# Queueing the small TensorE products of a hybrid decoder kernel and issuing them singly

## The chip, the cores and the metric

The kernel runs on one core of one Trainium2 chip. The metric is the device time of one execution in microseconds, of the slowest core (there is one). Three runs of the kernel before took 1936.96, 1938.45 and 1943.08 us; their median is 1938.45 us.

## The reference, cut to what matters

A trunk of two decoder layers over 1024 tokens of width 1024, in float32. Cut to its frame:

```python
for l in range(DEPTH):                       # DEPTH = 2
    h = x * (1 + scale1) + shift1            # scale, shift, gate: c_act @ ada_w[l]
    if l % 2 == 0:
        y = _even_mixer(h, ...)              # 4 gated-recurrence heads + windowed attention, 8 query heads
    else:
        y = _pool_mixer(h, ...)              # trailing means over 2, 4, 8, 16 tokens
    x = _layer_norm(ALPHA * x + g1 * y, ...)
    h = x * (1 + scale2) + shift2
    y = _conv_ffn(h, ...)                    # (silu(conv3(u)) * v) @ w_down, width 2816
    x = _layer_norm(ALPHA * x + g2 * y, ...)
```

The even mixer multiplies h by one input matrix, runs a chunkwise gated linear recurrence (128 keys by 128 values a head) and an attention over a window of 128 tokens beside each other, and maps both results by an output matrix.

## The kernel before, in words

The tokens are split in two halves of 512 (`NH = 2`, index `hf`), and each half in four tiles of 128 (`NT`). **Large products** are those with weights from memory. Each float32 operand is split into a high and a low part (`split`, L296 to L297: ACT casts the high part, DVE subtracts the low one), and three passes (`PASSES`) are summed in PSUM. They stand in `gemm` (L306, 128x512 each), `tok_products` (L430, 128x256), the value and gate part of `head_in` (L532, 128x256), `product` (L999, up-projection in a form with fewer products) and `down` (L1145).

**Small products** are those of 128x128 or less, in plain float32: in `mixer_head` the scores of a chunk at eight levels (`att`, L775, by `level`), transposes of the keys (`ktp`, L808), state updates (`up`, L817) and outputs (`ho`, L833 and L835); `join_head` transposes a head's output (`ogT`, L862); in `mixer_swa` transposes of keys, queries and probabilities (`kp` L636, `qp` L648, `tpz` L716); in `layer_norm` the variance (`varp`, L357, one column) and the transpose that spreads the reciprocal root (`rstd`, L365). Each comes in a group of four, one for each tile of 128 tokens or each head of a pair; `up` is three or four, `ho` four and then three or four. In the trace a small product of two operands is two MATMUL records and a transpose is one. The attention's scores (`sc`, L673) and values (`op`, L733) are small too, and the change leaves them as they are.

**The order of the work** is written out by hand with Python generators. A chain (`swa_chain`, one `head_chain` for each head and half, `norm_prep`, `between`, `last`) yields after each step; `start` puts it on the list `active` with a rate. The large products call `tick` at fixed places: in `gemm` after 9, 18 and (by `outproj` or `head_in`) 24 of 24 products, in the value part of `head_in` after each 24. At a tick every active chain gains its rate and takes one step for each whole unit: rate 1 for attention, 0.9 for a head, 3 for `norm_prep(0)`. A step places its group of four, and right behind it the DVE or ACT instruction that reads the result. The stages are: input projections of half 0, of half 1 (chains of half 0 beside them), `finish` for the chains of half 0, `outproj(0)` (192 large products, 24 ticks, chains of half 1 beside them), `finish` for those, `outproj(1)` with `norm_prep(0)` beside it, and then for each layer `early`, `paired`, `down(0)` and `down(1)`. `finish(gen)` runs what is left of a chain to its end, with nothing between.

The framework below the code places instructions on each engine by the code's order and by when it expects their operands, so an engine's order can differ from the code's. It sets all semaphores. PSUM is two pools of four banks: `mm` for large products, `ax` for small ones. Temporary tiles come from pools of 512 columns: `t2` (19 buffers) and `e2` (6).

Of the kernel before, what the change touches and what calls it, by code (L numbers as in the profile page):

```python
# [1 line left out]

# [1 line left out]

# [47 lines left out]
AHEAD = 2  # L52
KEEP = 5
PIN = 1
EARLY = (16, 22)
EARLY_CONV = (0, 12)
FILL = 0.65
# [4 lines left out]
def trunk(ctx: ExitStack, tc: tile.TileContext, a: dict, out: bass.AP):  # L62
# [34 lines left out]
    active = []  # L97

    def start(gen, rate):
        active.append([gen, rate, 0])  # L100
        return gen

    def tick():
        for item in list(active):
            item[2] += item[1]
            while item[2] >= 1:
                item[2] -= 1
                with ExitStack() as order:
                    for i in behind:
                        order.enter_context(tc.issue_after(i.ins))  # L110
                    over = next(item[0], active) is active
                if over:
                    active.remove(item)
                    break

    def finish(gen=None, keep=0):
        if gen is not None:
            for _ in gen:
                pass
            active[:] = [x for x in active if x[0] is not gen]  # L120
        else:
            while len(active) > keep:
                for _ in active.pop(0)[0]:
                    pass


    def load(name, shape, dt=F32, src=None):
# [197 lines left out]
    def layer_norm(r, w=HT, s=None):  # L325
        if s is None:
            s = t2("lns")[:, :w]
            V.tensor_tensor(s, r[0], r[1], ALU.add)
            for j in range(2, KT):
                yield  # L330
                V.tensor_tensor(s, s, r[j], ALU.add)
            yield
        mu = ax("mu")[:, :w]
        if w < HT:
            PE.matmul(mu, mean_w.bitcast(F32), s, start=True, stop=True)
        else:
# [19 lines left out]
        for tt in range(nt):  # L356
            PE.matmul(vp[:, tt : tt + 1], ss[:, tt * P : (tt + 1) * P], mean_c, start=True, stop=True)  # L357
# [6 lines left out]
        for tt in range(nt):  # L364
            PE.transpose(bp[:, tt * P : (tt + 1) * P], y[:, tt : tt + 1].broadcast_to([P, P]), ident)  # L365
        yield
        for j in range(KT):
            V.tensor_tensor(r[j], r[j], bp, ALU.mult)
            yield
# [58 lines left out]
    def tok_products(ps, w, h, k, t, first, last):  # L428
        for pi, (wi, hi) in enumerate(PASSES):
            PE.matmul(  # L430
                ps[t // 2][:, (t % 2) * 256 : (t % 2 + 1) * 256],
                h[k][:, hi, t * P : (t + 1) * P],
                w[wi][:, (k % 4) * 256 : (k % 4 + 1) * 256],
                start=first and pi == 0 and t % 2 == 0,
                stop=last and pi == 2 and t % 2 == 1,
            )

    def swa_tiles(hf):
        z = [b4(f"z{g}_{hf}").rearrange("p (t c) -> p t c", t=NT) for g in range(3)]
# [61 lines left out]
    def head_in(hd, hf, pf=None):  # L501
# [24 lines left out]
        for t in range(0, NT, 2):  # L526
            ps = mm("zt")
            for u in range(2):
                i = 0
                for k_ in range(KT):  # L530
                    for wi, hi in PASSES:
                        PE.matmul(  # L532
                            ps[:, u * 256 : (u + 1) * 256],
                            h[k_][:, hi, (t + u) * P : (t + u + 1) * P],
                            w[k_ // 4][wi][:, (k_ % 4) * 256 : (k_ % 4 + 1) * 256],
                            start=i == 0,
                            stop=i == 23,
                        )
                        i += 1
                if u == 0:  # L540
# [86 lines left out]
    def mixer_swa(z, hf):  # L627
# [4 lines left out]
        rope(z[1], 4, hf)  # L632
        yield
        kp = ax("kp")
        for t in range(NT):
            PE.transpose(kp[:, t * P : (t + 1) * P], z[2][:, t, 0:P], ident)  # L636
        kT = t2("kT")
        S.copy(kT, kp)
        kTs[hf], vv_ = kT, t2("vv").rearrange("p (t c) -> p t c", t=NT)
# [4 lines left out]
        yield  # L644
        def queries(t):
            qp = ax("qp")
            for j in range(4):
                PE.transpose(qp[:, j * P : (j + 1) * P], z[j // 2][:, t, (j % 2) * P : (j % 2 + 1) * P], ident)  # L648
            qT = t2("qT")
            S.copy(qT, qp)  # L650
            return qT
# [59 lines left out]
        def turn(t, kv, p):  # L711
            r = []
            for kb in (1,) if hf * NT + t == 0 else (0, 1):
                tpz = ax("tpz")
                for j in range(4):
                    PE.transpose(tpz[:, j * P : (j + 1) * P], p[:, j, kb * P : (kb + 1) * P], ident)  # L716
                pT = t2("pT")
                if kb:
                    V.tensor_copy(pT, tpz)
# [21 lines left out]
        qT = queries(0)  # L741
        yield
        for t in range(NT):
            cur = yield from scores(t, qT)
            yield
            if prev is not None:
                parts = turn(t - 1, 0, prev[0])
                yield
                parts += turn(t - 1, 1, prev[1])
                yield  # L750
            if t < NT - 1:
                qT = queries(t + 1)
# [5 lines left out]
        parts = turn(NT - 1, 0, prev[0])  # L758
        yield
        parts += turn(NT - 1, 1, prev[1])  # L760
        yield
        yield
        values(NT - 1, parts)
# [1 line left out]

    def mixer_head(st, hd, hf):
        f, K, q, Q, z = st
        tot = t2("tot")
        att = t2("att")

        def level(lhs, rhs):
            ps = ax("att")
            for c in range(NT):
                s = slice(c * P, (c + 1) * P)
                PE.matmul(ps[:, s], lhs[:, s], rhs[:, s], start=True, stop=True)  # L775
            return ps

        ps = level(K, q)
# [7 lines left out]
        cur, off = f, 0  # L786
        for li, m in enumerate(LEVELS):
            nb = HT // (2 * m)
            ps = level(K, Q)
# [14 lines left out]
            yield  # L804

        kp = ax("ktp")
        for c in range(NT):
            PE.transpose(kp[:, c * P : (c + 1) * P], K[:, c * P : (c + 1) * P], ident)  # L808
        kt = q
        S.copy(kt, kp)  # L810
        yield
        yield
        up = ax("up")
        for c in range(NT):
            if hf == NH - 1 and c == NT - 1:
                continue
            PE.matmul(up[:, c * P : (c + 1) * P], kt[:, c * P : (c + 1) * P], z[:, c, 0:P], start=True, stop=True)  # L817
        st_in = [states.get(hd)]
        for c in range(NT):
            if hf == NH - 1 and c == NT - 1:  # L820
# [7 lines left out]
        states[hd] = st_in[-1]  # L828
        yield
        op = ax("ho")  # L830
        for c in range(NT):
            s = slice(c * P, (c + 1) * P)
            PE.matmul(op[:, s], att[:, s], z[:, c, 0:P], start=True, stop=st_in[c] is None)  # L833
            if st_in[c] is not None:
                PE.matmul(op[:, s], Q[:, s], st_in[c], start=False, stop=True)  # L835
            if c == 1:
                yield
        ssq = sm([P, NT], "ssq", 2)
        junk = sm([P, P], "junk", 1)
        for c in range(NT):  # L840
# [16 lines left out]
    def join_head(hf, hd):  # L857
        o = o_hl[hf]
        ps = ax("ogT")
        for c in range(NT):  # L860
            s = slice(c * P, (c + 1) * P)
            PE.transpose(ps[:, s], og[hf, hd][:, s], ident)  # L862
        split(o[hd][:, 0, :], o[hd][:, 1, :], ps)

    def join_swa(hf):
# [13 lines left out]
    def head_chain(st, hd, hf):  # L879
        yield from mixer_head(st, hd, hf)  # L880
        yield
        while o_hl[hf] is None:
            yield
        join_head(hf, hd)
        yield

    rs_ = [None, None]
# [108 lines left out]
    def product(ps, w, blk, start, stop):  # L996
        for k in range(HK):
            for pi, (wi, hi) in enumerate(PASSES):
# [2 lines left out]
                    start=start and k == pi == 0, stop=stop and k == HK - 1 and pi == 2,  # L1001
                    skip_group_check=True,
                )
            if k == 1:
                tick()
        fill()
# [110 lines left out]
    def down(l, hf):  # L1117
# [15 lines left out]
        for j0 in range(0, KT, 2):  # L1133
# [4 lines left out]
            for c0, nk in CHUNKS[:2] if final else CHUNKS:  # L1138
                w = [weight("w_dn", l, hf, j, c0, nk) for j in (j0, j0 + 1)]
                for k in range(c0, c0 + nk):  # L1140
                    while len(g) < min(FP, k // 2 + 3):
                        load_hidden()
                    for jj in range(2):
                        for pi, (wi, hi) in enumerate(PASSES):
                            PE.matmul(  # L1145
                                ps[jj], w[jj][wi][:, (k - c0) * P : (k - c0 + 1) * P], act(k, hi),
                                start=k == pi == 0, stop=k == sum(last_k) - 1 and pi == 2,
                            )
                    tick()
                    if k % 4 == 3:  # L1150
                        fill()
# [220 lines left out]
```

## Time and profile before

| | |
|---|---|
| median of three runs | 1938.45 us |
| profiled execution | 1934.68 us |
| its span, first to last instruction | 1932.9 us |
| mean granted TensorE clock | 0.991 of full |
| PE busy | 1866.4 us (97%) |
| DVE busy | 1389.3 us (72%) |
| ACT busy | 897.4 us (46%) |

PE is TensorE's matmuls, PEld its weight loads, DVE is VectorE, ACT ScalarE. All durations below come from this one profiled execution, whose span is 1.8 us shorter than its own time. A matmul's recorded duration is modelled and overlaps that of the next one; the chain of waits gives each piece the time up to the next piece, and so shows what a group really takes on the engine.

### The profile page before, as it was taken

What the parts mean: (1) busy time and instruction counts of PE and PEld (TensorE: products, weight loads), DVE (VectorE), ACT (ScalarE), POOL (GpSimd) and SP (SyncE); (2) the same over time, 40 slices, a digit from 0 to 9 for tenths busy, and PEclk for the clock granted to TensorE, in tenths of its full rate; (3) what the DMA queues carried; (4) which work ended last, traced back from release to release, by engine and by line L of the source; (5) the groups of instructions that cost most, each with busy time, mean ns of one, the idle gap of its engine ahead of it and who ended that gap; (6) DMA issues with size and microseconds to landing.
All of it is one profiled execution on the core that took longest, in us unless ns stands there. A gap on an engine that the chain in (4) does not pass through costs nothing.

```text
span 1932.9 us, 25673 instructions
## 1 busy us (share of the span) xinstructions
PE 1866.4 (97%) x9390; PEld 1553.2 (80%) x9390; DVE 1389.3 (72%) x2651; ACT 897.4 (46%) x1408; POOL 0.2 (0%) x4
## 2 busy tenths in 40 slices
PE   6999999999998999999999999997999999999996
PEld 5988988898776888888888888885888888888886
DVE  6897677787789888887634784898887776634506
ACT  4764245433676444444522644656645443423522
POOL 0000000000000000000000000000000000000000
PEclk9999999999999999999999999998999999999998
DMA  8722332224777666554676757457644444867861
GB/s 312 243 96 87 110 110 94 92 100 143 248 264 281 236 222 236 205 180 153 234 271 231 279 176 275 145 186 272 231 151 152 147 155 154 286 232 255 321 213 44
DMA packets 139087, 377.98 MB, mean 196 GB/s; under 512 B 17104, under 2 KB 19536, under 8 KB 138960
## 3 DMA queue, kind: packets, MB, share of 16 engines
q1 hardware_dynamic: 126288, 353.78, 52.3%
q10 hardware_dynamic: 12672, 22.55, 3.1%
q8 instruction: 74, 1.21, 0.3%
q14 instruction: 53, 0.43, 0.1%
HBM read 289.24 MB, written 87.03 MB: 195 GB/s over the span
## 4 chain that ended last, share of the span: by engine, by line
PE 83%; DVE 8%; DMA 4%; ACT 2%; issue 2%; SPq 0%; DVEq 0%; ACTq 0%
PE pd L1145 23%; PE py L999 18%; PE pz L999 12%; PE px L999 9%; PE zt L532 4%; PE op L306 3%; PE att L775 3%; DMA adast<-in_ada_wT 2%; PE zt L430 2%; PE pd L306 2%; DVE whl L297 1%; PE aq L306 1%; PE pp L1231 1%; DVE adast L152 1%; PE af L306 1%
## 5 line engine op out<-in xcount | busy, mean ns | idle before, releaser
L999 PE MATMUL py<-t,whl 128*128 128x512 f32 x1584 | 374.5, 392 | 5.6 <-ACT whl L297 1.9
L999 PEld LDWEIGHTS py<-t,whl 128*128 128x128 f32 x1584 | 296.4, 188 | 75.6 <-DVE v L1109 3.3
L297 ACT CAST whl<-wst 128x1024 fp32r<-128x1024 f32 (+1 forms) x196 | 200.3, 1033 | 283.8 <-PE pd L1145 114.2
L1145 PE MATMUL pd<-gh,whl 128*128 128x512 f32 x1024 | 319.7, 390 | 0.0
L297 DVE TENSOR_TENSOR whl<-wst,whl 128x1024 fp32r<-128x1024 f32 (+1 forms) x196 | 233.1, 1199 | 104.8 <-ACT whl L297 104.1
L999 PE MATMUL px<-hf,whl 128*128 128x512 f32 x1056 | 254.0, 397 | 20.1 <-ACT uh L952 14.0
L999 PEld LDWEIGHTS px<-hf,whl 128*128 128x128 f32 x1056 | 201.0, 191 | 65.4 <-ACT uh L952 15.7
L1145 PEld LDWEIGHTS pd<-gh,whl 128*128 128x128 f32 x1024 | 192.0, 188 | 40.1
L1145 PE MATMUL pd<-gl,whl 128*128 128x512 f32 x512 | 199.4, 389 | 0.0
L152 DVE CUSTOM_DVE_ANT_0 adast<-adast,c 128x1024 f32<-128x1024 f32 x96 | 117.2, 1221 | 41.8 <-DMA adast<-in_ada_wT 41.5
L999 PE MATMUL pz<-t,whl 128*128 128x512 f32 x528 | 130.3, 395 | 0.0
L999 PE MATMUL pz<-hf,gs 128*128 128x512 f32 x528 | 129.1, 393 | 0.0
L999 PEld LDWEIGHTS pz<-t,whl 128*128 128x128 f32 x528 | 99.2, 188 | 23.6
L999 PEld LDWEIGHTS pz<-hf,gs 128*128 128x128 f32 x528 | 99.1, 188 | 22.7
L1145 PEld LDWEIGHTS pd<-gl,whl 128*128 128x128 f32 x512 | 96.1, 188 | 20.2
L1145 PE MATMUL pd<-gt,whl 128*128 128x512 f32 x432 | 103.3, 395 | 0.0
L532 PE MATMUL zt<-whl,h 128*128 128x256 f32 x768 | 100.6, 286 | 0.0
L953 ACT ACTIVATE uc<-uc 128x512 f32<-128x512 f32 x88 | 55.8, 634 | 91.9 <-DVE uc L948 76.1
L1155 DVE SCALAR_TENSOR_TENSOR r<-pd,mod,r 128x512 f32<-128x512 f32 x32 | 23.1, 750 | 104.6 <-PE pd L1145 104.6
L1145 PEld LDWEIGHTS pd<-gt,whl 128*128 128x128 f32 x432 | 80.7, 187 | 20.3 <-DVE gt L297 0.5
L946 DVE SCALAR_TENSOR_TENSOR uc<-u,cw,uc 128x511 f32<-128x511 f32 x124 | 92.4, 745 | 5.4 <-ACT uc L943 5.2
L532 PEld LDWEIGHTS zt<-whl,h 128*128 128x128 f32 x768 | 94.4, 191 | 0.7 <-issue 0.3
(244 smaller groups left out, 2694.9 us busy)
## 6 DMA issues: line engine op xcount, KB each, us to landing
wst<-in_w_up SPq DMA_DIRECT2D x126, 512.0 KB, 4.3
adast<-in_ada_wT SPq DMA_DIRECT2D x96, 512.0 KB, 3.9
wst<-in_w_dn SPq DMA_DIRECT2D x64, 512.0 KB, 5.6
wst<-g SPq DMA_DIRECT2D x44, 512.0 KB, 5.2
r<-r SPq DMA_DIRECT2D x64, 256.0 KB, 3.9
wl<-whl SPq DMA_DIRECT2D x32, 512.0 KB, 3.1
whl<-wl SPq DMA_DIRECT2D x32, 512.0 KB, 4.6
g<-uc SPq DMA_DIRECT2D x62, 256.0 KB, 2.0
```

The source lines that it names most:

```text
L152: V.tensor_tensor_reduce(out=w, in0=w, in1=cb, scale=1.0, scalar=0.0, op0=ALU.mult, op1=ALU.add, accum_out=col(mods[l, ch], k),)
L297: return S.copy(hi, src), V.tensor_tensor(lo, src, hi.bitcast(F32), ALU.subtract)
L306: PE.matmul(ps, w[wi][:, k * P : (k + 1) * P], act(k, hi), start=i == 0, stop=i == n - 1)
L430: PE.matmul(ps[t // 2][:, (t % 2) * 256 : (t % 2 + 1) * 256], h[k][:, hi, t * P : (t + 1) * P], w[wi][:, (k % 4) * 256 : (k % 4 + 1) * 256 ...
L532: PE.matmul(ps[:, u * 256 : (u + 1) * 256], h[k_][:, hi, (t + u) * P : (t + u + 1) * P], w[k_ // 4][wi][:, (k_ % 4) * 256 : (k_ % 4 + 1) * ...
L775: PE.matmul(ps[:, s], lhs[:, s], rhs[:, s], start=True, stop=True)
L946: V.scalar_tensor_tensor(uc[:, sh:], u[:, : HT - sh], cw, uc[:, sh:], ALU.mult, ALU.add)
L953: S.activation(uc, uc, AF.Silu)
L999: PE.matmul(ps, w[wi][:, k * P : (k + 1) * P], blk[k][hi], start=start and k == pi == 0, stop=stop and k == HK - 1 and pi == 2, skip_group ...
L1145: PE.matmul(ps[jj], w[jj][wi][:, (k - c0) * P : (k - c0 + 1) * P], act(k, hi), start=k == pi == 0, stop=k == sum(last_k) - 1 and pi == 2,)
L1155: V.scalar_tensor_tensor(n[j], ps[jj], col(mods[l, 5], j), n[j], ALU.mult, ALU.add)
L1231: PE.matmul(ps, wg[wi][:, b : b + P], o[k][:, hi, :], start=i == 0, stop=i == 5)
```

## The change

A step that has small products hands them to a queue (`spread`, `small`), and the chain stands still until they are out. Every large product calls `slip`; at every second one (`GAP = 2`) `slip` issues one small product from the head of the queue, which all chains share. When a chain's last queued product is out, `slip` takes the chain's next step at once, so that the reader of the result follows directly; the step after that waits for a tick, as before. `tick` passes by chains with products in the queue. `finish` empties the queue first (`flush`), and in it the products come out in a row, as before.

Queued are: `varp`, `rstd`, `kp`, `qp`, `tpz`, `att`, `ktp`, `up`, `ho` (all of a head in one go, without the yield after the second chunk) and `ogT`. Two tiles of each head of half 0 (`tot`, `att`) move from the pool `t2` to `e2`. Nothing that is computed changes, and no instruction is added on an engine.

```diff
+GAP = 2
...
     def start(gen, rate):
-        active.append([gen, rate, 0])
+        active.append([gen, rate, 0, 0])
         return gen
+
+    def step(item):
+        now[:] = [item]
+        with ExitStack() as order:
+            for i in behind:
+                order.enter_context(tc.issue_after(i.ins))
+            over = next(item[0], active) is active
+        now.clear()
+        if over:
+            active.remove(item)
+        return not over
...
     def tick():
         for item in list(active):
+            if item[3]:
+                continue
             item[2] += item[1]
-            while item[2] >= 1:
+            while item[2] >= 1 and not item[3]:
                 item[2] -= 1
...
+                if not step(item):
                     break
 
     def finish(gen=None, keep=0):
+        flush()
         if gen is not None:
             for _ in gen:
-                pass
+                flush()
...
+    small = []
+    passed = [0]
+
+    def slip():
+        passed[0] += 1
+        if small and passed[0] >= GAP:
+            passed[0] = 0
+            item = issue()
+            if not item[3] and item in active:
+                step(item)
+
+    def issue():
+        f, item = small.pop(0)
+        f()
+        item[3] -= 1
+        return item
+
+    def flush():
+        while small:
+            issue()
+
+    def spread(work):
+
+        item = now[0] if now else [None, 0, 0, 0]
+        item[3] = len(work)
+        small.extend((f, item) for f in work)
+        while item[3]:
+            yield
...
                 PE.matmul(ps, w[wi][:, k * P : (k + 1) * P], act(k, hi), start=i == 0, stop=i == n - 1)
                 i += 1
+                slip()
...
     def mixer_head(st, hd, hf):
         f, K, q, Q, z = st
-        tot = t2("tot")
-        att = t2("att")
+        tot, att = (t2("tot"), t2("att")) if hf else (e2("tot"), e2("att"))
 
         def level(lhs, rhs):
             ps = ax("att")
-            for c in range(NT):
-                s = slice(c * P, (c + 1) * P)
-                PE.matmul(ps[:, s], lhs[:, s], rhs[:, s], start=True, stop=True)
+            cuts = [slice(c * P, (c + 1) * P) for c in range(NT)]
+            yield from spread([
+                partial(PE.matmul, ps[:, s], lhs[:, s], rhs[:, s], start=True, stop=True) for s in cuts
+            ])
             return ps
...
```

`slip()` also follows each product in `tok_products`, in the value part of `head_in`, in `product` and in `down`. The other groups named above are changed in the manner of `level`.

## Rows read from the trace of the kernel before

**Rows 1.** Busy time by engine, whole span: us, share, instructions.
```profile
PE 1866.4 (97%) x9390; PEld 1553.2 (80%) x9390; DVE 1389.3 (72%) x2651; ACT 897.4 (46%) x1408; POOL 0.2 (0%) x4
```

**Rows 2.** Stretches: from:to, length, busy PE, PEld, DVE, ACT, POOL, clock, DMA, GB/s.
```profile
110.00:490.00 380.00, 374.93 (x2528) 326.13 (x2528) 291.21 (x793) 156.70 (x342) 0.00 (x0) 1.00 0.31 107
...
515.00:550.00 35.00, 35.00 (x155) 28.70 (x154) 30.98 (x52) 22.09 (x36) 0.00 (x0) 0.96 0.57 195
```

**Rows 3.** Chain of waits, 400 to 484: start, us, piece (products in a row).
```profile
407.71 0.44 PE ktp L808 x4
408.14 2.07 PE op L306 x9
410.21 0.89 PE att L775 x8
...
481.54 0.79 PE varp L357 x8
```

**Rows 4.** Chain of waits, 263 to 264: transposes in a pair and singly.
```profile
263.50 0.22 PE ogT L862 x2
263.71 0.24 PE aq L306
263.95 0.12 PE ogT L862
```

**Rows 5.** What PE waited for, 62 to 500: us in total, times, longest.
```profile
PE ho L833 <- DVE st L826: 1.7, 1, 1.7
PE ogT L862 <- DVE og L854: 0.9, 1, 0.9
PE tpz L716 <- ACT pT L721: 0.9, 1, 0.9
PE att L775 <- DVE o L297: 0.6, 1, 0.6
```

**Rows 6.** Chain of waits, 242 to 249: small groups beside 128x256 products.
```profile
242.76 1.16 PE att L775 x8
...
247.66 0.62 PE ktp L808 x4
```

**Rows 7.** Chain of waits, 436 to 456: the last head's end on PE.
```profile
436.95 0.44 PE ktp L808 x4
...
440.84 0.67 PE up L817 x6
...
446.53 0.22 PE ho L835 x2
```

**Rows 8.** Timeline of DVE and ACT, 437 to 464: the last head's end, the norm's start.
```profile
437.42 0.59 ACT L810 COPY q<-ktp 128x512 f32<-128x512 f32 x1 [4.50 <-PE ktp L808]
...
441.54 1.11 DVE L826 SCALAR_TENSOR_TENSOR st<-st,tot,up 128x128 f32<-128x128 f32 x3 [0.42 <-PE up L817]
...
448.46 0.17 DVE L842 TENSOR_SCALAR ssq<-ssq 128x4 f32<-128x4 f32 x1 [0.25 <-ACT junk L841]
...
450.84 1.13 DVE L854 SCALAR_TENSOR_TENSOR og<-ho,rmsy,f 128x128 f32<-128x128 f32 x4
...
454.85 0.68 DVE L297 TENSOR_TENSOR o<-ogT,o 128x512 fp32r<-128x512 f32 x1
...
463.64 0.75 DVE L898 SCALAR_TENSOR_TENSOR r<-op,mod,r 128x512 f32<-128x512 f32 x1 [2.21 <-PE op L306]
```

**Rows 9.** Chain of waits, 490 to 514: from the norm to the up-projection.
```profile
491.57 4.87 DVE r L368 x8
...
504.30 5.37 DMA r<-in_xT
```

**Rows 10.** Timeline of PE, 509 to 520: after the idle time.
```profile
512.72 0.73 PE L999 MATMUL px<-hf,whl 128*128 128x512 f32 x2 [3.47 <-ACT whl L297]
513.98 6.21 PE L999 MATMUL px<-hf,whl 128*128 128x512 f32 x19 [0.53 <-DVE whl L297]
```

More of the change, by code (lines that the diff above doesn't have):

```diff
@@ L1 @@
 from contextlib import ExitStack
+from functools import partial
 import numpy as np
@@ L99, in start @@
     def start(gen, rate):
-        active.append([gen, rate, 0])
+        active.append([gen, rate, 0, 0])
         return gen
+    def step(item):
[8 more added lines that the diff above has]
+        return not over
+    now = []
     def tick():
         for item in list(active):
+            if item[3]:
+                continue
             item[2] += item[1]
-            while item[2] >= 1:
+            while item[2] >= 1 and not item[3]:
                 item[2] -= 1
[L108 to L113, printed above, removed]
+                if not step(item):
                     break
     def finish(gen=None, keep=0):
+        flush()
         if gen is not None:
             for _ in gen:
-                pass
+                flush()
             active[:] = [x for x in active if x[0] is not gen]
@@ L355, in layer_norm @@
         vp = ax("varp")
-        for tt in range(nt):
-            PE.matmul(vp[:, tt : tt + 1], ss[:, tt * P : (tt + 1) * P], mean_c, start=True, stop=True)
+        yield from spread([
+            partial(PE.matmul, vp[:, tt : tt + 1], ss[:, tt * P : (tt + 1) * P], mean_c, start=True, stop=True)
+            for tt in range(nt)
+        ])
         v = sm([P, NT], "lnv")[:, :nt]
@@ L363, in layer_norm @@
         bp = ax("rstd")[:, :w]
-        for tt in range(nt):
-            PE.transpose(bp[:, tt * P : (tt + 1) * P], y[:, tt : tt + 1].broadcast_to([P, P]), ident)
+        yield from spread([
+            partial(PE.transpose, bp[:, tt * P : (tt + 1) * P], y[:, tt : tt + 1].broadcast_to([P, P]), ident)
+            for tt in range(nt)
+        ])
         yield
@@ L634, in mixer_swa @@
         kp = ax("kp")
-        for t in range(NT):
-            PE.transpose(kp[:, t * P : (t + 1) * P], z[2][:, t, 0:P], ident)
+        yield from spread([
+            partial(PE.transpose, kp[:, t * P : (t + 1) * P], z[2][:, t, 0:P], ident) for t in range(NT)
+        ])
         kT = t2("kT")
@@ L646, in queries @@
             qp = ax("qp")
-            for j in range(4):
-                PE.transpose(qp[:, j * P : (j + 1) * P], z[j // 2][:, t, (j % 2) * P : (j % 2 + 1) * P], ident)
+            yield from spread([
+                partial(
+                    PE.transpose, qp[:, j * P : (j + 1) * P], z[j // 2][:, t, (j % 2) * P : (j % 2 + 1) * P], ident
+                )
+                for j in range(4)
+            ])
             qT = t2("qT")
@@ L714, in turn @@
                 tpz = ax("tpz")
-                for j in range(4):
-                    PE.transpose(tpz[:, j * P : (j + 1) * P], p[:, j, kb * P : (kb + 1) * P], ident)
+                yield from spread([
+                    partial(PE.transpose, tpz[:, j * P : (j + 1) * P], p[:, j, kb * P : (kb + 1) * P], ident)
+                    for j in range(4)
+                ])
                 pT = t2("pT")
@@ L788, in mixer_head @@
             nb = HT // (2 * m)
-            ps = level(K, Q)
+            ps = yield from level(K, Q)
             view = lambda t, i: t.rearrange("p (b two m) -> p b two m", two=2, m=m)[:, :, i, :]
@@ L806, in mixer_head @@
         kp = ax("ktp")
-        for c in range(NT):
-            PE.transpose(kp[:, c * P : (c + 1) * P], K[:, c * P : (c + 1) * P], ident)
+        yield from spread([
+            partial(PE.transpose, kp[:, c * P : (c + 1) * P], K[:, c * P : (c + 1) * P], ident) for c in range(NT)
+        ])
         kt = q
@@ L813, in mixer_head @@
         up = ax("up")
[L814 to L817, printed above, removed]
+        yield from spread([
+            partial(
+                PE.matmul, up[:, c * P : (c + 1) * P], kt[:, c * P : (c + 1) * P], z[:, c, 0:P], start=True, stop=True
+            )
+            for c in range(NT - (hf == NH - 1))
+        ])
         st_in = [states.get(hd)]
@@ L830, in mixer_head @@
         op = ax("ho")
+        work = []
         for c in range(NT):
             s = slice(c * P, (c + 1) * P)
-            PE.matmul(op[:, s], att[:, s], z[:, c, 0:P], start=True, stop=st_in[c] is None)
+            work.append(partial(PE.matmul, op[:, s], att[:, s], z[:, c, 0:P], start=True, stop=st_in[c] is None))
             if st_in[c] is not None:
-                PE.matmul(op[:, s], Q[:, s], st_in[c], start=False, stop=True)
-            if c == 1:
-                yield
+                work.append(partial(PE.matmul, op[:, s], Q[:, s], st_in[c], start=False, stop=True))
+        yield from spread(work)
         ssq = sm([P, NT], "ssq", 2)
@@ L859, in join_head @@
         ps = ax("ogT")
-        for c in range(NT):
-            s = slice(c * P, (c + 1) * P)
-            PE.transpose(ps[:, s], og[hf, hd][:, s], ident)
+        cuts = [slice(c * P, (c + 1) * P) for c in range(NT)]
+        yield from spread([partial(PE.transpose, ps[:, s], og[hf, hd][:, s], ident) for s in cuts])
         split(o[hd][:, 0, :], o[hd][:, 1, :], ps)
```

24 lines of the change are left out of this document (15 added, 9 removed).

## The prediction

> **What bounds the kernel now.** I read the busy times first: PE is busy for 97% of the span and DVE for 72% [rows 1]. The stretches then show where that is loose: through the mixer, 110 to 490 us, PE is busy for 374.9 of 380 us, at the full clock [rows 2]. So the small products can give back time in two ways only: by taking less of PE, or by sparing the few waits in front of them. The chain of waits prices them, since it gives each piece the time up to the next one. Nine large products take 2.07 us, 0.23 each. Four score products, eight records, take 0.89 us; four transposes 0.44; four variance products of a single column, again eight records, 0.79 [rows 3]. So a record costs about 0.11 us, and nearly as much with one column as with 128: a group pays for its weight loads, one after another.
>
> **Part 1: singles in place of groups.** The queue carries 568 products of the mixer by the loops (160 of attention, 51 for each of eight heads) and 64 of the norms. Does one that stands alone cost less? The trace has the case: the four transposes of one head came out as one, two and one between large products, since their operands came one by one. Setting aside the first, which waited, the pair took 0.22 us and the single 0.12, with a large product of 0.24 between [rows 4]. Three records took 0.34, against 0.33 by the group's price. The step is therefore worth nothing, or a loss of about 4 ns a product, in the mixer 568 x 4 ns = 2.3 us. I take the 2.3, because the neighbouring large products are slower by as much, and keep 0 as the other end.
>
> The Trainium skill ("TensorE: Matmul & The Clock Gate", "Step-by-step: what each phase is for") says that a weight load is pulled ahead under the matmul that is running. That is the rule by which a lone small product would get its load for nothing. Rows 4 don't bear it out as a gain: the load of the large product that follows then lies bare instead. By that rule the sum would be the second rival's.
>
> **Part 2: waits in front of small products.** PE waited 4.1 us in all for operands of products that will be queued, in four waits [rows 5]. More hides in stretched groups: 1.16 us where scores take 0.89, 0.62 where transposes take 0.44 [rows 6]. That is 0.18 to 0.27 a group, and some fifteen groups beside the 128x256 products may be so, 4 us. The upper bound of a gain is 8 us. A spread group reaches the reader of its result later, and its chain goes on at the next tick, so dependent groups of a head stand no further apart than before: by the loops about 3 us from the last product of a level to the first of the next, before and after. The wait of the first product of a group stays. I take a quarter of the 8, 2 us, and keep 0 and 8.
>
> **Part 3: the chains get longer.** This is the part that I hold for decisive. A level takes a tick before: 6 to 9 large products. After, its four products take some 8 large products to come out, and only then is the next tick counted: about 15 to 17 together. A head has 13 steps with products, and the last head of half 1 has only the 192 large products of `outproj(0)` to run beside; 13 x 15 = 195. The queue has 192 / 2 = 96 places there, and 51 products of this head and over 40 of the older chains, which lag, want them. Followed through the loops, the last head has just queued its key transposes (`ktp`) when `outproj(0)` ends. Its states, outputs, norm and transpose are then run in a row by `finish`, ahead of `outproj(1)`, whose fourth block of weights needs that head's result.
>
> What that costs: before, the stretch from `ktp` to the split result took from 436.95 to 455.5 us, ticks included, and was over 8 us before PE came to `outproj(1)` (the last sum of `outproj(0)` starts on DVE at 463.64) [rows 7, 8]. Run without ticks it takes: ACT copy 0.59, three updates 0.67, states 1.11, outputs 8 x 0.22 = 1.76, ACT squares 1.7 (from the end of the outputs, 446.75, to the first DVE step, 448.46), small DVE steps to the end of `og` 448.46 to 451.97 = 3.5, transposes 0.44, the split's two parts 0.6 and 0.68; 11.0 us in all [rows 3, 7, 8]. PE has in that time its own 0.67 + 1.76 + 0.44 = 2.9 us and nine large products before the missing block, 2.1 us [rows 3]. That leaves 6.0 us bare if the rest stays in order. But the order isn't that of the code: `varp` stands on PE at 481.54, with large products around it that the code places behind it [rows 3]. With four banks for large sums, the first nine products of three more output blocks, 27 x 0.23 = 6.2 us, can go ahead and cover it. I take the cover as there.
>
> What isn't covered is DVE. From 463.64 to the end of the norm's scaling at 496.4 it has the norm of half 0, on which the start of `early` hangs: scaling, then transfers of the residual, then casts of weights [rows 8, 9]. Into that stretch come the last head's states, small steps, `og` and split, 1.11 + 3.5 + 0.68 = 5.3 us. The stretch starts 2.9 us earlier, as those products left the stage before. So 2.4 us, with 0 and 5.3 as ends. SP's queue gets the same transfers in the same order; the residual's load that ends at 509.7 moves with the tiles that the norm frees [rows 9].
>
> **Part 4: norms of the later stages.** Their `varp` and `rstd` go by readiness: the rest of the group is placed 6 large products, 1.4 us, after its first, if that is ready at its place at all. I cost it at nothing, since PE has large products to issue meanwhile; uncovered, it would be two groups x 1.4 us for each of the seven full norms, of which those that a stage's start waits for, two or three, count: up to 8 us. The two half norms at the end run in `finish` or at a high rate, much as before. The move of two tiles to `e2` costs nothing: no instruction changes, and half 0's heads are through before `outproj(0)` takes that pool.
>
> **The sum.** +2.3 - 2.0 + 2.4 = +2.7 us against the profiled 1934.68, which is 3.8 us under the median. Put on the median of 1938.45 it gives 1941 us. A measurement of this kernel can tell about 0.3%, 5.8 us, from no change; the forecast is inside that.
>
> **Rivals.**
>
> *Waits vanish (faster).* The queue makes first products late enough that the 8 us of part 2 go, single products cost nothing more, and the last head's end is hidden wholly: 1938.45 - 8 = 1930.5. For it: rows 6 show stretched groups where the 128x256 products are dense, and there chains will be slower. Against it: the first of a group waits as before. 0.22.
>
> *Loads are hidden (faster).* One record of each queued product costs only its columns, a quarter of a large product, 0.057, in place of 0.11: 568 x 54 ns = 31 us, 1908 us. Against it are rows 4; for it only that they are one case of transposes. 0.03.
>
> *The last head in order (slower).* Nothing is taken forward in `outproj(1)`, so PE stands bare for 6.0 us there. The clock falls after such a stop: after 3.47 us of idle time 19 products took 6.21 us, against 4.4 at 0.23, and the granted clock of the stretch behind was 0.96 [rows 2, 10]. With 1.9 us for that, 2.3 for the singles and nothing spared: 1938.45 + 10.2 = 1948.7. It decides from about 4 us of bare wait on. For it: by the loops that head is late by some 11 us of dependent steps. Against it: the shuffled order. 0.25. The norms' 8 us of part 4 would end at the same place, 1946; I give it 0.06.
>
> *The change does not do what it says.* Products not ready at their place are put off, and a queued group comes out together after all, as `rstd` does where the norm is late: 1938.5. 0.06.
>
> **How the numbers follow.** Forecast 0.38, no effect 0.06: no change 0.44. Faster 0.22 + 0.03 = 0.25. Slower 0.25 + 0.06 = 0.31. The likeliest is 1941, with 1933 to 1946 as its own range (ends of parts 1 to 3). The range of eight in ten reaches to 1926, somewhat beyond the vanished waits, as earlier states shift other waits too, and to 1954, the late head with DVE's 5.3 us on top.
>
> **What would show it.** Right: single `att` products (two records) between pairs of large ones, each record still some 0.11 us; `ho` and `ogT` of the last head after the end of `outproj(0)`, and large products of several output blocks among them; the norm's scaling on DVE (491.57 before) later against PE's stage. Wrong: single products visibly under 0.2 us for two records (then the second rival); a wait of PE for the last head's split of over 4 us, with a granted clock under 1 behind it (the third); waits in front of `att` gone from 215 to 250 us (the first); or a change outside the mixer and the norms, which no step here accounts for.

## The result, and the profile after

The changed kernel took 1951.24 us (median of four runs, 1950.49 to 1952.78) beside 1938.14 us for the kernel before on the same chip: a ratio of 1.0066, interval 1.0049 to 1.0084. A second set gave 1953.85 against 1939.10 us, 1.0079 (1.0059 to 1.0099). So the change costs 13 to 15 us. That is inside the range of the prediction (1926 to 1954), but above what its likeliest case allowed (1941, own range 1933 to 1946): a slower kernel had a chance of 0.31, and no measurable change, its first choice, 0.44.

The profiled execution took 1952.78 us (before: 1934.68). First the busy line of its page, which answers to [rows 1].

```profile
PE 1879.4 (96%) x9390; PEld 1553.5 (80%) x9390; DVE 1393.7 (71%) x2651; ACT 905.6 (46%) x1414; POOL 0.2 (0%) x4
```

Then the windows of the same execution that answer to [rows 2], with the same columns.

```profile
110.00:490.00 380.00, 376.22 (x2522) 322.36 (x2521) 285.18 (x780) 169.01 (x366) 0.00 (x0) 1.00 0.30 105
515.00:550.00 35.00, 29.70 (x118) 22.42 (x118) 30.58 (x45) 27.10 (x42) 0.00 (x0) 0.95 0.67 226
```

The section on the change says that no instruction is added on an engine. For ACT that isn't so: it has 1414 in place of 1408. The six are loads of its function tables (`ACT_TABLE_LOAD`, 27 in place of 21, 1.28 us each). They stand where exponentials of the attention and sigmoids of the heads follow each other, which they do more often in the new order. e8 takes them up again.

Through the mixer, where the change was made, PE is as full as before: 376.2 of 380 us in place of 374.9. Most of the loss shows behind it: from 515 to 550 us PE is busy for 29.7 us, where it was busy for all 35. (The two windows start at different work: before, the 3.47 us in which PE stood idle ahead of the up-projection end just before 515 [rows 10].) The queue itself does what it says. The timeline of PE (start, us, engine, line, tiles, idle time in front) shows the scores between pairs of large products:

```profile
414.55 0.38 PE L153 MATMUL att<-q,k 128*128 128x128 f32 x2
414.69 0.71 PE L349 MATMUL op<-o,whl 128*128 128x512 f32 x2
415.23 0.39 PE L153 MATMUL att<-q,k 128*128 128x128 f32 x2
415.37 0.71 PE L349 MATMUL op<-o,whl 128*128 128x512 f32 x2
```

From one score product to the next it takes 0.68 us: two large products at 0.23 and 0.22 for the two small records. That is the price in a group [rows 3], 0.11 a record. Now the end of the last head of half 1 on PE, which answers to [rows 7]:

```profile
461.69 0.27 PE L153 MATMUL ktp<-ident,k 128*128 128x128 f32 x1
...
464.97 0.94 PE L153 MATMUL up<-zh,q 128*128 128x128 f32 x6
...
467.77 0.39 PE L153 MATMUL ho<-st,q 128*128 128x128 f32 x2
467.91 5.49 PE L349 MATMUL op<-o,whl 128*128 128x512 f32 x23
474.06 0.30 PE L153 MATMUL ogT<-ident,og 128*128 128x128 f32 x1 [0.66 <-DVE og L914]
...
475.83 2.36 PE L349 MATMUL op<-o,whl 128*128 128x512 f32 x9 [0.21 <-ACT o L340]
```

It is 25 us late (`ktp` at 461.7, 436.95 before), but PE hardly waits for it: 23 large products go ahead, and 0.66 and 0.21 us are left bare. DVE is another matter. Its timeline, against [rows 8] and [rows 9]:

```profile
463.38 0.75 DVE L957 SCALAR_TENSOR_TENSOR r<-op,mod,r 128x512 f32<-128x512 f32 x1 [3.13 <-PE op L349]
...
469.85 0.17 DVE L902 TENSOR_SCALAR ssq<-ssq 128x4 f32<-128x4 f32 x1 [2.42 <-ACT junk L901]
...
473.57 1.13 DVE L914 SCALAR_TENSOR_TENSOR og<-ho,rmsy,f 128x128 f32<-128x128 f32 x4
474.61 0.68 DVE L372 TENSOR_TENSOR lns<-r,r 128x512 f32<-128x512 f32 x1
...
506.59 4.87 DVE L416 TENSOR_TENSOR r<-r,rstd 128x512 f32<-128x512 f32 x8 [0.74 <-PE rstd L153]
```

The first sum of the norm of half 0 (`lns`) stands directly behind the last head's `og`, at 474.61 us. Before, it stood at 455.44, and the norm's sums were added while `outproj(0)` still ran. In between DVE is idle for 3.13 and for 2.42 us, with seven of the eight residual sums ready from 458.1 us on. The norm's first sum comes 11.2 us after the last residual sum starts (463.38). The norm's scaling starts at 506.59 in place of 491.57. From there the delay reaches PE. PE's waits between 490 and 650 us (total, times, longest):

```profile
PE px L1058 <- DVE r L957: 5.5, 3, 2.6
PE px L1058 <- ACT s L1099: 4.3, 3, 2.6
PE py L1058 <- DVE v L1169: 2.9, 1, 2.9
```

The timeline of PE at the first two of them and at the longest:

```profile
516.20 3.01 PE L1058 MATMUL px<-hf,whl 128*128 128x512 f32 x12 [2.58 <-DVE r L957]
521.18 4.62 PE L1058 MATMUL px<-hf,whl 128*128 128x512 f32 x12 [1.97 <-DVE r L957]
...
637.73 4.61 PE L1058 MATMUL py<-t,whl 128*128 128x512 f32 x12 [2.92 <-DVE v L1169]
```

The first two waits are for `r` (L957), the residual sums of half 1, which read `outproj(1)`'s results out of the banks that the up-projection wants. The chain of waits (start, us, piece) shows what holds the sum up at the second one. DVE is not busy; it is idle for 2.17 us before that sum. The sum needs a load of the residual from memory, and this load stands behind the late norm's scaled result, which is first written out (SPq L983). The lines answer to [rows 9]:

```profile
506.59 4.87 DVE r L416 x8
...
514.86 0.32 SPq L983
...
515.24 4.45 DMA r<-in_xT
...
519.71 0.64 ACT r L954
...
520.37 0.76 DVE r L957
...
521.18 4.63 PE px L1058 x12
```

It is the second of four such loads and starts at 515.24 us; before, the second started at 504.30 [rows 9], 10.9 us earlier. Behind some of these waits the granted clock was lower too, by windows 0.57 of full, mostly 1.2 GHz in place of 2.4:

```profile
522.00:526.00 4.00, 3.79 (x10) 2.48 (x8) 3.42 (x6) 3.84 (x6) 0.00 (x0) 0.57 1.00 329
597.00:601.00 4.00, 4.00 (x12) 3.11 (x11) 4.00 (x8) 3.48 (x7) 0.00 (x0) 0.57 1.02 353
638.00:642.00 4.00, 4.00 (x12) 3.10 (x12) 3.76 (x6) 1.78 (x3) 0.00 (x0) 0.57 0.73 234
```

The clock does not explain the difference between the kernels, though: over the stretch C of the next section it is 0.98 in both profiles of the changed kernel, and 0.99 and 0.97 in the two of the kernel before (the last section has the windows). What grew there is PE's idle time: 17.3 and 15.7 us, against 13.0 and 11.2.

### The profile page after: what moved, and what is told of

The parts are those of the page before. It is cut to its first block, busy times and chain, and to the rows that moved or that the text cites. A ratio compares the mean times of both kernels' runs of the same rounds, so it can differ in the third digit from the quotient of the medians.

```text
span 1951.0 us, 25664 instructions
## 1 busy us (share of the span) xinstructions
PE 1879.4 (96%) x9390; PEld 1553.5 (80%) x9390; DVE 1393.7 (71%) x2651; ACT 905.6 (46%) x1414; POOL 0.2 (0%) x4
## 4 chain that ended last, share of the span: by engine, by line
PE 77%; DVE 11%; DMA 8%; ACT 2%; issue 2%; SPq 0%; DVEq 0%; ACTq 0%
PE pd L1205 22%; PE py L1058 16%; PE pz L1058 11%; PE px L1058 7%; PE op L349 4%; PE zt L581 3%; PE att L153 3%; DMA wst<-in_w_up 2%; PE zt L478 2%; DVE whl L340 2%; DMA adast<-in_ada_wT 2%; PE pd L349 2%; PE aq L349 2%; PE af L349 2%; PE pp L1292 1%
## 5 line engine op out<-in xcount | busy, mean ns | idle before, releaser
L1058 PE MATMUL px<-hf,whl 128*128 128x512 f32 x1056 | 259.1, 401 | 21.9 <-ACT uh L1011 9.7
L581 PE MATMUL zt<-whl,h 128*128 128x256 f32 x768 | 123.2, 301 | 0.0
L349 PE MATMUL op<-o,whl 128*128 128x512 f32 x384 | 106.4, 411 | 0.2 <-ACT o L340 0.2
L581 PEld LDWEIGHTS zt<-whl,h 128*128 128x128 f32 x768 | 103.7, 191 | 3.2 <-issue 2.8
```

What stands on the lines that cost most here:

```text
L581: PE.matmul(ps[:, u * 256 : (u + 1) * 256], h[k_][:, hi, (t + u) * P : (t + u + 1) * P], w[k_ // 4][wi][:, (k_ % 4) * 256 : (k_ % 4 + 1) * ...
L1058: PE.matmul(ps, w[wi][:, k * P : (k + 1) * P], blk[k][hi], start=start and k == pi == 0, stop=stop and k == HK - 1 and pi == 2, skip_group ...
```

## The experiments

Two executions of one kernel differ by several us, so stretches between the same two large products are compared. The program issues 8064 of them in the same order in every version. In the table A runs from the 337th to the 600th (67 to 128 us before), B to the 1921st, the first of `outproj(1)`, C from there to the 2700th, in `paired(0)`, and D from the 5400th to the 5700th, from `early(1)` into `paired(1)`. "Scaling" is how long after the start of `outproj(1)` the norm's scaling of half 0 begins on DVE. All are us of the profiled execution; the ratio is of the timed runs.

| kernel | ratio (interval) | A | B | C | D | scaling |
|---|---|---|---|---|---|---|
| before | | 60.9 | 335.5 | 198.4 | 79.3 | 28.1 |
| before, again | 0.9999 (0.9985 to 1.0013) | 63.4 | 337.2 | 200.7 | 80.9 | 28.1 |
| after | 1.0066 (1.0049 to 1.0084) | 62.6 | 333.8 | 211.6 | 84.6 | 43.4 |
| after, again | 1.0079 (1.0059 to 1.0099) | 66.2 | 334.0 | 209.8 | 85.7 | 43.1 |
| late head without a queue (e3) | 1.0047 (1.0032 to 1.0062) | 61.1 | 332.0 | 210.8 | 79.9 | 42.3 |
| after, last head at once (e2) | 1.0042 (1.0028 to 1.0056) | 65.1 | 336.6 | 202.5 | 84.0 | 28.3 |
| after, norms at once (e4) | 1.0079 (1.0066 to 1.0093) | 65.2 | 334.6 | 213.9 | 80.0 | 43.1 |
| after, norm of half 0 first (e6) | 1.0062 (1.0042 to 1.0083) | 65.9 | 333.7 | 207.7 | 83.2 | 30.1 |
| after, last head and norms at once (e8) | 1.0022 (1.0013 to 1.0032) | 63.3 | 336.7 | 199.2 | 79.5 | 28.3 |
| only the norms queued (e9) | 1.0028 (1.0017 to 1.0039) | 59.5 | 336.4 | 201.6 | 83.0 | 28.1 |
| GAP 1 (e1) | 1.0011 (1.0000 to 1.0023) | 64.5 | 336.0 | 200.6 | 81.1 | 28.2 |
| GAP 1, last head at once (e7) | 0.9990 (0.9977 to 1.0003) | 62.1 | 334.1 | 200.5 | 79.4 | 28.2 |
| the same again | 1.0003 (0.9993 to 1.0014) | 63.9 | 335.1 | 199.3 | 81.7 | 28.3 |
| GAP 1, last head and norms at once (e10) | 1.0005 (0.9993 to 1.0017) | 62.4 | 335.4 | 199.7 | 80.8 | 28.2 |

**The first four** were to tell my theory (the late head holds up the norm) from the price of queued products in the mixer (rival a) and in the norms (rival b).

*e1: one queued product after every large one.*

```diff
-GAP = 2
+GAP = 1
```

> The changed kernel with one queued product after every large one (GAP = 1). My theory (the last head of half 1 ends late, and the norm of half 0 stands behind it in DVE's order): groups come out in half the large products, the head's og leaves DVE's stretch of the norm earlier, so a part of the 13 us comes back: 1938 to 1945 us, and the norm's first sums on DVE stand nearer to 455 than to 474 us. Rival a (the queued products themselves cost time on PE): 1950 as before, or more, since the products are only packed closer. Rival b (norms' queued varp and rstd): norms have other work between them too, only half as long: about 1945, but with the norm of half 0 still starting at 474.

1940.96 us against 1938.78. The sums of the norm begin at 461.5 us, 3.1 us behind `og` and ahead of the end of `outproj(0)`, the scaling is back at 28.2 us, and C at 200.6. As the theory had it, and against rival a; against rival b it is the norm's early start that speaks.

*e2: the last head of half 1 issues its groups at once.*

```diff
+plain = []
 def spread(work):
     item = now[0] if now else [None, 0, 0, 0]
+    if now and now[0][0] in plain:
+        for f in work:
+            f()
+        return
...
     gens.append(start(head_chain(st, hd, hf), R_HEAD))
+    if hf == 1 and hd == 3:
+        plain.append(gens[-1])
```

> The changed kernel, but the chain of the last head of half 1 alone issues its groups at once; everything else stays queued. My theory: that head ends before the norm of half 0 again, the norm's first sums on DVE go back to about 455 to 460 us, and nearly all of the 13 us comes back: 1937 to 1943 us. Rivals a and b (queued products of the rest of the mixer, or of the norms): 51 of 632 products change, so 1949 to 1951 us.

1947.57 us: a miss. DVE's timeline shows that the mechanism went as expected:

```profile
458.34 1.12 DVE L920 SCALAR_TENSOR_TENSOR og<-ho,rmsy,f 128x128 f32<-128x128 f32 x4
462.85 0.68 DVE L378 TENSOR_TENSOR lns<-r,r 128x512 f32<-128x512 f32 x1
...
499.35 4.87 DVE L422 TENSOR_TENSOR r<-r,rstd 128x512 f32<-128x512 f32 x8 [0.81 <-PE rstd L153]
```

Scaling is back at 28.3 us after the start of `outproj(1)`, and C at 202.5 us. But 8.8 us remain: A and D are as long as in the changed kernel. The late head is not all. (The eight runs scatter widely, from 1942.8 to 1951.3 us, and the profiled one is the slowest.)

*e3: the kernel before, with the last head alone started at a lower rate.*

```diff
-gens.append(start(head_chain(st, hd, hf), R_HEAD))
+gens.append(start(head_chain(st, hd, hf), 0.38 if hf == 1 and hd == 3 else R_HEAD))
```

> The kernel before, with no queue at all, but the last head of half 1 started at rate 0.38 in place of 0.9, so that its key transposes come at the end of the stage of outproj(0) and the rest in a row, as in the changed kernel. My theory: the same loss with no queue, the norm's first sums at about 470 us or later, 1947 to 1953 us. Rivals a and b: 1937 to 1940 us, as the kernel before.

1947.80 us, as the theory said, and with no queue. The order on DVE is that of the changed kernel:

```profile
471.59 1.13 DVE L854 SCALAR_TENSOR_TENSOR og<-ho,rmsy,f 128x128 f32<-128x128 f32 x4
472.63 0.68 DVE L328 TENSOR_TENSOR lns<-r,r 128x512 f32<-128x512 f32 x1
...
503.47 4.87 DVE L368 TENSOR_TENSOR r<-r,rstd 128x512 f32<-128x512 f32 x8
```

C takes 210.8 us (198.4 and 200.7 before), while A and D are as before. The lateness alone is worth 9 us of the whole.

*e4: the norms' `varp` and `rstd` at once (`at_once` issues a group in a row), the mixer queued.*

```diff
-        yield from spread([
+        yield from at_once([
             partial(PE.matmul, vp[:, tt : tt + 1], ss[:, tt * P : (tt + 1) * P], mean_c, start=True, stop=True)
...
-        yield from spread([
+        yield from at_once([
             partial(PE.transpose, bp[:, tt * P : (tt + 1) * P], y[:, tt : tt + 1].broadcast_to([P, P]), ident)
```

> The changed kernel, but varp and rstd of the norms are issued at once, as before; the mixer stays queued. My theory: the lateness is there before the norm's first product, so 1948 to 1952 us. Rival b (the queued varp and rstd hold the norms up by up to 8 us): 1940 to 1944 us.

1954.78 us, above what either said. In its profile the loss of D is gone (80.0 us against 84.6 and 85.7), so rival b has a place in the trace. The time isn't lower, as C takes 213.9 us, 2 to 4 us more than in the changed kernel. The clock accounts for that much in this profile: over C the granted clock is 0.96 in place of 0.98. By the trace some 17 us of C are at 1.2 GHz in place of 10, and 7 us more at half the rate cost 3 to 4 us.

**The next four.** *e6: the norm's first steps ahead of the rest of the last head.*

```diff
     outproj(0)
+    np0 = norm_prep(0)
+    for _ in range(KT + 1):
+        next(np0)
     for g in b_gens:
         finish(g)
-    pa_ = start(norm_prep(0), R_NP)
+    pa_ = start(np0, R_NP)
```

> The changed kernel with the queue as it is; only the first steps of the norm of half 0 (its sums, its split and its mean product) are placed ahead of what is left of the last head of half 1, so that DVE takes them as the last residual comes. My theory (the loss comes from the norm's place behind the last head's end on DVE): the norm's scaling goes from 507 us back to 490 to 497, and of the 13 us 8 or more come back: 1938 to 1943 us. Rival: the last head's lateness itself holds PE or the queue; then the head ends later still, since DVE serves the norm first, PE waits for its last split, and the time stays at 1948 us or over.

1951.12 us: the rival's outcome. On DVE the norm did go first, and the scaling came at 30.1 us:

```profile
466.87 0.69 DVE L375 TENSOR_TENSOR lns<-lns,r 128x512 f32<-128x512 f32 x1
479.88 1.13 DVE L914 SCALAR_TENSOR_TENSOR og<-ho,rmsy,f 128x128 f32<-128x128 f32 x4
...
496.05 4.86 DVE L416 TENSOR_TENSOR r<-r,rstd 128x512 f32<-128x512 f32 x8
```

But the head's `og` came 13 us behind the last sum, and now PE stands still for it. PE's waits, 455 to 650 us:

```profile
PE ogT L153 <- DVE og L914: 2.9, 1, 2.9
PE op L349 <- ACT whl L340: 2.2, 1, 2.2
...
PE op L349 <- ACT o L340: 0.7, 1, 0.7
```

The first and the third of these are the head's, 3.6 us; the second is the last block of `outproj(1)` waiting for its weights. So my theory was too narrow. The late head is the cause of C's growth; the order on DVE decides only which of two stages pays, the norm or `outproj(1)`. C is 207.7 us here, 3 less than in the changed kernel.

*e7: GAP 1 and the last head at once (the edits of e1 and e2 together).*

> The changed kernel with one queued product after every large one and the last head of half 1 issued at once: the queue without the late head. This is the test of the single products' own price. My prediction's part 1 said +2.3 us for them and part 2 -2.0: so 1938 to 1942 us. If single products cost or save more than that, it lies outside.

1936.24 us beside 1939.10, below the expected 1938 to 1942, and, run again,

> The run with one queued product after every large one and the last head issued at once, again unaltered: 1935 to 1940 us. The question is whether the 2.9 us below the kernel before repeat; if the singles are worth nothing, the two runs together give a ratio within 0.9985 and 1.0005.

1940.86 beside 1938.94, just over the expected 1940. The first was under the kernel before and the second over it; both intervals hold 1, and the two ratios lie within the 0.9985 to 1.0005 that was asked. So with one after every large product, and no chain that ends late, small products that stand alone are worth nothing that can be measured, net of the waits that they spare.

*The two kernels again, unaltered.*

> The changed kernel again, unaltered: 1949 to 1953 us. Its profile is to show what repeats: the step of 12 us or more between the start of outproj(1) and the start of paired(0) should be there again; the extra 4 us around the start of paired(1) should not, if it belongs to that one execution.

> The kernel before again, unaltered, for a second profile of it: 1935 to 1942 us. What differs between two profiles of the same kernel is the size below which no place in the changed kernel's trace can be read.

Medians of 1953.85 us, 0.9 over what was expected, and 1938.71 us. The long C repeats (209.8 against 200.7), and D does too (85.7 against 80.9). I had expected D's part to be chance of one execution, and it was not. A's part I had not looked at before. A wait of the attention's scores for DVE (`mxs`) stands there, on PE's timeline of the changed kernel's second profile:

```profile
106.55 2.07 PE L728 MATMUL sc<-kT,qT 64*128 64x256 f32 x6 [2.15 <-DVE mxs L737]
```

And on that of the kernel before's second profile:

```profile
101.31 1.13 PE L673 MATMUL sc<-kT,qT 64*128 64x256 f32 x6 [1.25 <-DVE mxs L682]
```

Behind the longer wait the six products take 2.07 us in place of 1.13: the clock of that stretch, by windows, was

```profile
105.00:112.00 7.00, 5.45 (x22) 4.62 (x23) 6.53 (x24) 0.63 (x1) 0.00 (x0) 0.56 0.75 259
```

In the kernel before's second profile the clock fell as well, only for a shorter time and just behind the six products: it is 0.66 from 102 to 107 us. A lower clock in A therefore comes and goes between profiles, and A has to be read with it. From 95 to 140 us the clock is 0.92 in four of the six profiles with the mixer queued at `GAP = 2` (A 65.1 to 66.2 us) and 1.00 in the other two (62.6 and 63.3). With `GAP = 1` it is 0.96 in two (64.5 and 63.9) and 1.00 in two (62.1 and 62.4); with no queue in the mixer 0.96 in one (63.4) and 1.00 in three (59.5 to 61.1). So at the full clock A is about 2 us longer with a queue, whichever `GAP`, and 2 to 3 us more where the clock fell.

**The last three** were to complete the account.

*e8: the edits of e2 and e4 together.*

> The changed kernel with one queued product after every second large one, but the last head of half 1 and the norms' varp and rstd issued at once. My account now has two causes: the late last head (some 11 us between the start of outproj(1) and paired(0)) and the queued varp and rstd of the norm beside early(1) (3 to 5 us at the start of paired(1)). With both undone nothing of the 13 us should be left: 1936 to 1941 us. If the queue costs anything else, in the mixer itself, it shows here as a time of 1943 us or more.

1944.37 us, 5.4 us over the kernel before: a miss, over the line of 1943 that stood for a further cost in the mixer. C (199.2) and D (79.5) are as before, so both causes are undone. What is left is the queue at every second large product in the rest of the mixer. Where it costs is open. In its profile none of the four stretches is longer than in both profiles of the kernel before; A is 63.3 us, but with `GAP = 1` A is as long (62.1 to 64.5) at no cost in the whole. One rival was not tested: the six further table loads of ACT stand in B in all six profiles whose mixer is queued at `GAP = 2`, and in none of the other eight. B is not longer by them in the two (e2, e8) whose last head is in time (336.6 and 336.7 us, against 335.5 and 337.2 before), so no loss is seen where they stand, but no run separates them from the queue.

*e9: all of the mixer at once, only `varp` and `rstd` queued (`spread` replaced by `at_once` in the mixer).*

> All products of the mixer issued at once and only the norms' varp and rstd queued, one after every second large product. My account: the last head is in time, so nothing is lost between outproj(1) and paired(0) but what the norms themselves are late; at the start of paired(1) 3 to 5 us are lost: 1941 to 1945 us. Rival (the second loss comes from the late head too, or from chance): 1937 to 1940 us.

1944.38 us, as expected, 5.4 us over the kernel before: D takes 83.0 us, and A and B are not longer. The profiled execution was the fastest of the twelve (1938.98 us), so its stretches can't show the whole 5.4; its D is 2.9 us over the mean of 80.1 before. D is 83.0 to 85.7 us in all five profiles whose norms are queued at `GAP = 2`, and 79.3 to 81.7 in the other nine. PE's wait in D, by the waits of the changed kernel:

```profile
PE py L1058 <- ACT u L1157: 2.3, 1, 2.3
```

The same wait of PE in e9:

```profile
PE py L1063 <- ACT u L1162: 1.1, 1, 1.1
```

In e4 and e8, with the norms at once, that wait isn't there.

*e10: GAP 1, last head and norms at once.*

> One queued product after every large one, the last head of half 1 and the norms issued at once. If the shorter queue spared the norms already, this equals the run with only the last head at once: 1935 to 1939 us. If the norms' products at that spacing still cost something, it is faster than that run by up to 2 us.

1939.54 us, 1.0005 (0.9993 to 1.0017), half a us over the 1939 that was expected. With a product after every large one the norms' queue costs nothing more. No version that was tried is measurably faster than the kernel before.

## Why the prediction was right, and where it was wrong

The means of two profiles each put the loss in its places: C 210.7 - 199.6 = 11.1, D 85.2 - 80.1 = 5.1, A 64.4 - 62.2 = 2.2, B 333.9 - 336.4 = -2.5, the rest together 0.1. That is 16 us, as the four profiled executions differ (1955.98 - 1939.94); the medians of the runs say 13 to 15. The forecast of 2.7 us was too small by 10 to 12. That its range held is in part luck: the upper end, 1954, was the third rival's bare PE with DVE's 5.3 us on top, while the time was lost in three places, of which one was costed too low, one at nothing and one as a gain.

**Part 3 failed, in its DVE term.** Its first half came true: by the loops the last head had just queued its key transposes when `outproj(0)` ended, and `ktp` came out at 461.7 to 463.2 us with `outproj(1)` starting at 463.2. The cover on PE held too: 23 large products went ahead, 0.9 us were bare in place of the 6.0 of the third rival. The step that failed is "So 2.4 us, with 0 and 5.3 as ends". It added the head's work to DVE's load in the norm's stretch, as if the norm could start as before and only share the engine. In fact the norm's sums were placed behind the head's last step and waited for the whole dependent chain, idle time included: the first came 11.2 us after the last residual sum, and the scaling 15 us later against `outproj(1)` than before. I had that chain's length, 11.0 us, in the paragraph before and held it against PE alone. From the scaling on, the path was the one that I had named: the residual's load, 10.9 us later. C grew by 11.1, but that this is near the chain's 11.0 is chance: about 2.9 us of C are the head's own products, which left B (-2.5), so 8.2 were lost. 4.4 of them are PE's idle time; the rest lies in its busy time, and was not split further. e3 shows that this lateness needs no queue, e2 and e1 that it goes when the head is in time, e6 that placing the norm first only moves the wait to PE.

**Part 4 failed in size.** I costed the norms' queue at nothing, with 8 us as the end. D shows 5.1 us for the norm beside `early(1)`, with a wait of 2.3 and 3.1 us in the two profiles; behind it the clock stayed full in the first (1.00 from 1389 to 1393 us) and fell in the second (0.63 from 1395 to 1399). Alone (e9) it costs 5.4 us of the whole. With the late head present, grouping the norms gave nothing back (e4); in its profile a lower clock in C took up what D gave. The parts are not additive: late head (e3) 9.0, norms (e9) 5.4 and the rest (e8) 5.4 would be 19.8 us.

**Part 2's gain did not come.** The wait of `ho` that [rows 5] show (1.7 us) is gone, as the queue's slower chains would have it, and PE's idle time in B fell from 5.1 and 5.5 us to 2.9 and 3.1. But the scores of the attention wait 2.3 us for DVE, 0.9 before, and in A the idle time rose from 1.7 and 2.9 us to 3.6 and 4.9: what was spared in one stretch was lost in the other. With both other causes undone e8 is still 5.4 us slower, and the mechanism of this rest is open; which step of DVE holds the scores up was not tried, nor were the table loads.

**Part 1 was right.** A lone product of two records takes 0.22 us, as in a group, and the three runs with GAP 1 and the last head at once, which also keep whatever waits they spare, lie at 0.9990 to 1.0005; the 2.3 us that I took would be 1.0012, which two of the three intervals hold; nothing, the other end, lies in all three. The rival of hidden loads (1908 us) is refuted with it. The Trainium skill ("TensorE: Matmul & The Clock Gate", "Step-by-step: what each phase is for") says that a weight load is pulled ahead under the running matmul. Here the pair of records between two large products takes what it takes in a group, and no gain is seen.

Of the rivals, "the last head in order" came nearest by its time (1948.7) and by its cause, a late head, but not by its mechanism: PE did not stand bare for the head (0.9 us), and the time went by DVE's order and the late norm. Its picture is nearer to what e6 shows, where PE does stand bare for the head, for 3.6 us. That the change would do nothing, or spare waits, was refuted by the first timeline above and by the ratio.

## What to carry to other kernels

When work is spread out, count first what the last chain before a deadline has left: its steps times the new step length, and the places in the queue. Where it ends late, do not add its work to another engine's load; ask what stands behind its last step in that engine's order, since DVE here waited for the whole chain with other work ready. And compare executions stretch by stretch between the same instructions, twice for each kernel: a loss in three places looks like one in the total.

## What the runs showed of the hardware that was not expected

Idle times as short as 2 to 3 us in front of PE were followed by a granted clock of half (0.56 and 0.57 in the windows above), three times in the 130 us behind 515. The kernel before has such a stretch once there in its first profile, behind 3.47 us [rows 10], and three times in its second, behind waits of 3.38, 2.13 and 1.99 us:

```profile
519.00:523.00 4.00, 3.90 (x10) 3.08 (x11) 4.00 (x6) 2.67 (x3) 0.00 (x0) 0.57 0.50 157
587.00:591.00 4.00, 4.00 (x12) 3.14 (x11) 4.00 (x8) 2.07 (x4) 0.00 (x0) 0.57 1.02 398
625.00:632.00 7.00, 5.87 (x14) 4.62 (x15) 3.51 (x4) 1.68 (x4) 0.00 (x0) 0.51 0.96 351
```

So the same kernel, at the same places, runs at either level from one execution to the next. It isn't certain for a given wait either: behind 2.12 us at the place of the second of these the kernel before's first profile kept the full clock (1.00 from 583 to 592 us), and after 2.27 us in front of the scores the first profile of the changed kernel kept it too (1.00 from 95 to 140 us), while after 2.15 us at the same place the second fell to 0.56.
